# Tail of an MLP down projection: last token pair's products in another order, sample rows' norm first, one more row's affine on GpSimd, last row's norm from bn_stats moments

## The chip, the cores and the metric

The kernel runs on one core of one Trainium2 chip. The metric is device time in microseconds of one execution. A core has five engines that work side by side, each with its own queue of instructions in order: TensorE (PE, with its weight loads shown as PEld), VectorE (DVE), ScalarE (ACT), GpSimd (POOL) and SyncE (SP, which here issues the DMAs). They wait for each other through semaphores.

## The reference, cut to what matters

One layer of a streaming encoder for 1024 prompt rows and 64 sample rows of width 1024: a mixer of three head groups, a norm, and a squared-ReLU MLP with a second norm. The change touches only the end of the last line:

```python
def layer_norm(x, g, b):
    mu = jnp.mean(xf, axis=-1, keepdims=True)
    var = jnp.mean(jnp.square(xf - mu), axis=-1, keepdims=True)
    return ((xf - mu) * lax.rsqrt(var + LN_EPS) * g + b)
...
        h = jnp.square(jax.nn.relu(jnp.einsum('btd,df->btf', x, w_up)))
        xp = layer_norm(ALPHA * xp + h @ w_down, ln2_g[l], ln2_b[l])
```

The outputs concerned are y_prompt (1024 x 1024) and y_sample (64 x 1024), in float32.

## The kernel before, in words

The down projection multiplies the 4096 hidden features by w_down. The features are worked off in 16 groups g of 256. The 1024 prompt rows are eight tiles t of 128 rows, and a tile's sum stands in SBUF as acc[t, half], two halves of 512 columns. Tiles t and t + 4 form a pair, and a pair's two row tiles by two column halves are made of seven block products instead of eight (a Strassen-like scheme): the class Down has product(n) for n = 0 to 6, six matmuls of 128x128 by 128x512 each (L1715), with results in three PSUM banks named A, B and D. The tuple DOWN gives each product's bank: 0 A, 1 B, 2 A, 3 D, 4 A, 5 D, 6 A. Products in one bank add up, so a bank is read by evac(n) after each product, and the next product in the same bank has to wait until that read is done. evac(0) copies A to a tile p on ACT (L1732). evac(1) adds B and p to half 0 of tile i (its final value), evac(2) adds A to half 1 of i, evac(3) adds D to half 1 of i + 4, evac(4) finishes half 1 of i + 4, evac(5) half 1 of i, evac(6) half 0 of i + 4. The adds run on DVE (L1682). B starts from half 0 of tile i, copied there by preload() on ACT (L1703).

The last two groups, 14 and 15, form the tail. There are four Downs, ch[0] to ch[3]: ch[0] has tiles 0 and 4, ch[1] tiles 1 and 5 (group 14), ch[2] tiles 2 and 6, ch[3] tiles 3 and 7 (group 15). In the tail a final add is one instruction that also gives the row sums (L1725, a custom DVE operation and a short read of its accumulator). do(k, n) issues product n of ch[k] and its evac. h_split makes the high and low parts of a block of hidden features: per half of it two copies on ACT (L1421, L1425) and a subtraction on DVE (L1426).

When a tile is final, its norm follows. In order these are, by helper: neg_mean(t) on DVE (L1789); squares(t), a pass over 1024 columns on ACT with a sum (L1794) and then two small operations on POOL (L1784 and L1785, scale and offset, then the power -1/2); shift(t) on POOL (L1805). Then the affine, in one of two ways. normalize(t) on ACT (L1809), times(t) on POOL (L1813, by g) and plus(t) on POOL (L1817, plus b) with a DMA of the rows out (L1818). Or on_dve(t, i, step): for half i, step 0 is (y + (-mean)) * g (L1825) and step 1 is y * rstd + b with the DMA out (L1827, L1828), where g and b come from four PSUM tiles gbp that put_gb() fills on ACT (L1942). The sample rows are row tile NB = 8; fold(half) adds their two partial sums (L1950 on ACT, L1952 on DVE), moments are bn_stats (L1776) and scale does bn_aggr (L1781) and POOL operations (L1782, L1785), then shift (L1803).

The tail's order is written out by hand: the context in_order() ties each engine's instructions to the order in which the statements stand. So an instruction that waits holds back all that was written after it for its engine.

Which rows go which way before: tiles 8, 0, 4 and 1 wholly through ACT and POOL; of tile 2 columns 512 to 1023 and of tile 7 columns 768 to 1023 so; tiles 5, 6, 3 and the rest of 2 and 7 on DVE. ch[3] runs its products as 0, 1, 2, 3, 4, 5, 6.

## Time and profile before

| | us |
|---|---|
| time, median of 3 runs | 1411.81 (1410.02 to 1411.91) |
| time of the profiled execution | 1411.73 |
| its span, first to last instruction | 1410.0 |
| PE busy in the span | 1328.1 (94%) |
| DVE, ACT, POOL busy | 1002.6, 718.5, 602.3 |
| PE, DVE, ACT, POOL busy in the window 1385 to 1395 | 9.05, 7.63, 8.63, 8.51 |
| PE, DVE, ACT, POOL busy in the window 1400 to 1410 | 0.00, 5.92, 2.73, 3.59 |

The span is what the profile covers; the time of the same execution is 1.7 us longer. All places in time below are microseconds from the span's start. A row of the timeline gives the start of an instruction (or of several alike, with their count), its duration, engine, line and operation, what it writes and reads, and in square brackets how long its engine stood idle before it and which engine's instruction ended that. On the whole the kernel is bound by PE, but the tail is not: the last matmul ends some 11 us ahead of the span's end.

### The profile page before, as it was taken

Reading aid. Unit: us, or ns where it says so; the run is one execution under the profiler, and the core shown is the slowest. Engines: PE = TensorE matmul, PEld = TensorE weight load, DVE = VectorE, ACT = ScalarE, POOL = GpSimd, SP = SyncE. Lnnn points to the kernel's source line nnn. Section 1 sums busy time; section 2 is a strip of 40 time slices with the busy share of each in tenths; the row PEclk is TensorE's granted clock in tenths of the full one; section 3 lists DMA queues with packets and bytes.
Section 4 is the critical chain, followed back from the end, with each engine's and each line's share of the span. In section 5 each row is a group of like instructions: output and inputs, shape, how many; then the busy total and the mean of one; then the engine's idle time right before and its main releaser. Section 6 shows DMA issues by size and latency. Waiting matters only on the chain.

```text
span 1410.0 us, 24288 instructions
## 1 busy us (share of the span) xinstructions
PE 1328.1 (94%) x8827; PEld 1206.8 (86%) x8827; DVE 1002.6 (71%) x1799; ACT 718.5 (51%) x1561; POOL 602.3 (43%) x663
## 2 busy tenths in 40 slices
PE   7999999999989997999989999999979999999996
PEld 6899999999888986866889999999967787777774
DVE  3577565676786599887866768767678777667777
ACT  3366565666665485333423323232247667667675
POOL 3222222266565535654411122212166665654657
PEclk9999999999999998999999999999999999999999
DMA  7324242322313434422234434344558344344343
GB/s 218 77 78 113 58 117 65 81 63 56 80 27 83 127 91 135 132 105 68 76 110 140 153 133 139 117 166 139 173 187 295 99 160 165 118 136 150 101 135 128
DMA packets 149217, 168.87 MB, mean 120 GB/s; under 512 B 27100, under 2 KB 115484, under 8 KB 149096
## 3 DMA queue, kind: packets, MB, share of 16 engines
q1 hardware_dynamic: 149096, 167.30, 37.9%
q8 instruction: 70, 1.15, 0.3%
q14 instruction: 51, 0.42, 0.1%
HBM read 109.26 MB, written 51.71 MB: 114 GB/s over the span
## 4 chain that ended last, share of the span: by engine, by line
PE 63%; DVE 12%; ACT 7%; DMA 6%; POOL 6%; issue 5%; SPq 1%; DVEq 0%; ACTq 0%; POOLq 0%
PE zA L1264 9%; PE A L1715 6%; PE zD L1264 6%; PE mx L244 5%; PE kvsb L355 5%; PE kvfox L355 4%; PE D L1715 3%; PE zC L1264 3%; PE zB L1264 3%; DVE snsb L538 2%; DMA raw<-w_in 2%; PE qfox L496 2%; PE Sfox L554 2%; DMA rd<-w_down 2%; PE ptfox L602 1%
## 5 line engine op out<-in xcount | busy, mean ns | idle before, releaser
L97 POOL TENSOR_TENSOR wa<-wr,wa 128x512 fp32r<-128x512 f32 x42 | 63.8, 1548 | 228.5 <-ACT wa L1204 228.5
L97 POOL TENSOR_TENSOR wd<-rd,wd 128x512 fp32r<-128x512 f32 x77 | 101.1, 1322 | 121.2 <-ACT wd L1204 116.9
L244 PE MATMUL mx<-xT,oTb 128*128 128x512 f32 (+1 forms) x416 | 108.0, 412 | 1.6 <-ACT oTb L202 1.5
L1264 PE MATMUL zD<-xo,ws 128*128 128x288 f32 (+1 forms) x720 | 98.1, 289 | 0.6 <-DVE h4a L1426 0.3
L1264 PE MATMUL zA<-xo,ws 128*128 128x288 f32 (+1 forms) x720 | 98.1, 290 | 0.0
L244 PEld LDWEIGHTS mx<-xT,oTb 128*128 128x128 f32 (+1 forms) x416 | 78.1, 193 | 21.7 <-ACT oTb L202 2.5
L1264 PEld LDWEIGHTS zD<-xo,ws 128*128 128x128 f32 x720 | 93.7, 189 | 1.1 <-DVE h4a L1426 0.5
L1264 PEld LDWEIGHTS zA<-xo,ws 128*128 128x128 f32 x720 | 94.1, 189 | 0.1
L540 POOL TENSOR_TENSOR sgsb<-sgsb,snsb 128x127 f32<-128x127 f32 (+7 forms) x48 | 58.8, 1227 | 78.8 <-DVE snsb L538 64.3
L355 PE MATMUL kvfox<-wkvfox,xT 128*128 128x256 f32 (+3 forms) x624 | 90.6, 294 | 1.5 <-ACT wkvfox L331 0.5
L1204 ACT ACTIVATE wd<-rd 128x512 fp32r<-128x512 f32 x105 | 63.8, 624 | 51.6 <-DMA rd<-w_down 25.8
L355 PE MATMUL kvsb<-wkvsb,xT 128*128 128x256 f32 (+1 forms) x624 | 87.7, 286 | 0.0
L1715 PE MATMUL A<-wd,wd 128*128 128x512 f32 x312 | 83.0, 401 | 2.5 <-DVE acc L1682 2.3
L355 PEld LDWEIGHTS kvfox<-wkvfox,xT 128*128 128x128 f32 (+1 forms) x624 | 81.6, 193 | 3.3 <-DVE xT L97 1.0
L1396 POOL TENSOR_TENSOR rd<-rd 128x512 f32<-128x512 f32 x56 | 78.9, 1409 | 10.9 <-DVE b L97 8.7
L538 DVE TENSOR_TENSOR_SCAN snsb<-snsb,one 128x128 f32<-128x128 f32 (+7 forms) x48 | 72.2, 1507 | 13.3 <-ACT snsb L537 12.5
L1275 ACT ACTIVATE sn<-zA 128x256 f32<-128x256 f32 (+1 forms) x80 | 31.0, 390 | 98.4 <-PE zA L1264 82.6
L355 PEld LDWEIGHTS kvsb<-wkvsb,xT 128*128 128x128 f32 (+1 forms) x624 | 79.2, 187 | 0.2
L1715 PEld LDWEIGHTS A<-wd,wd 128*128 128x128 f32 x312 | 58.9, 191 | 18.9 <-DVE acc L1682 4.2
L1715 PE MATMUL A<-wd,h4a 128*128 128x512 f32 x240 | 65.1, 395 | 0.4 <-DVE acc L1682 0.3
L1478 ACT ACTIVATE ws<-wr 128x1024 fp32r<-128x1024 f32 x28 | 29.0, 1057 | 54.0 <-DVE wr L1214 54.0
L1715 PEld LDWEIGHTS A<-wd,h4a 128*128 128x128 f32 x240 | 44.5, 188 | 12.6 <-ACT p L1732 1.2
(537 smaller groups left out, 3746.2 us busy)
## 6 DMA issues: line engine op xcount, KB each, us to landing
h_dr<-hh SPq DMA_DIRECT2D x30, 512.0 KB, 3.2
rd<-w_down SPq DMA_DIRECT2D x30, 512.0 KB, 4.5
awa<-h_dr SPq DMA_DIRECT2D x30, 512.0 KB, 4.5
wr<-w_up SPq DMA_DIRECT2D x14, 1024.0 KB, 5.4
hr<-h_dr SPq DMA_DIRECT2D x32, 384.0 KB, 3.6
h_dr<-hh SPq DMA_DIRECT2D x30, 384.0 KB, 3.9
raw<-w_in SPq DMA_DIRECT2D x44, 256.0 KB, 3.3
xr<-x_prompt SPq DMA_DIRECT2D x8, 512.0 KB, 7.2
```

What stands on the lines that cost most here:

```text
L97: eng.tensor_tensor(out, src, hi.bitcast(F32), op=ALU.subtract)
L244: nc.tensor.matmul(acc[0:m], oT[:, k, hx, 0:m], wo[k // 4][hw][:, k % 4, cs], start=(i == 0), stop=(i == len(seq) - 1))
L355: nc.tensor.matmul(acc[0:n, c0:c0 + n1 - n0], xT[k // 4][:, k % 4, c:c + n], wt[:, k, hw, n0:n1], start=(i == 0), stop=(i == len(seq) - 1))
L496: nc.tensor.matmul(acc[:, 0:w], wq[:, k, hw, :], xT[k // 4][:, k % 4, c:c + w], start=(i == 0), stop=(i == len(seq) - 1))
L538: nc.vector.tensor_tensor_scan(g[:, 0:n][:, ::-1], g[:, 0:n][:, ::-1], one.broadcast_to([P, n]), 1.0, op0=ALU.mult, op1=ALU.bypass)
L540: nc.gpsimd.tensor_tensor(s[:, 0:n - 1], s[:, 0:n - 1], g[:, 1:n], op=ALU.mult)
L1204: nc.scalar.activation(hi, raw, AF.Copy)
L1264: nc.tensor.matmul(z, w[:, hw, k], xop(s, bo, hx)[:, k, :], start=(new and k == 0 and j == 0), stop=(k == 3 and j == 2), skip_group_check= ...
L1275: nc.scalar.activation(c, z, AF.Copy)
L1396: eng.tensor_tensor(r[:, o], r[:, x], r[:, y], op=ALU.subtract)
L1478: nc.scalar.activation(ws[:, 0, q, c], src[:, q], AF.Copy)
L1715: nc.tensor.matmul(z, h[:, hx, q, o], wset[self.c % 2][q][:, hw, wb], start=((n in (0, 3) or n == 1 and self.c == 0) and q == 0 and j == 0 ...
```

## The change

- ch[3] runs its products as 0, 3, 1, 2, 5, 4, 6, with the norm work of other tiles put at other places between them.
- The sample rows: fold, moments, scale and shift stand ahead of do(0, 3) instead of behind it and do(0, 4), and normalize, times and plus directly behind do(0, 4); the split of group 14's second block and the loads of group 15's second part come after the fold.
- Tile 0: normalize and times stand ahead of squares(4).
- Tiles 1 and 5: squares and normalize are placed earlier, among h_split's instructions. Tile 5 goes wholly through ACT and POOL (normalize, times, plus) instead of four on_dve steps, and put_gb() now stands behind normalize(5).
- Tile 3: columns 512 to 1023 go through normalize, times and plus instead of on_dve.
- Tile 7: its final adds are plain additions without row sums; instead of neg_mean and squares it has bn_stats per half on DVE, bn_aggr, and the POOL operations of the sample rows; on_dve then subtracts the mean.

```diff
             def last(self, at, z, other=None):
...
-                if self.sums is None:
+                if self.sums is None or t == NB - 1:
                     add(False, acc[at], z, other)
...
             if step == 0:
-                nc.vector.scalar_tensor_tensor(y, y, st[:, 12:13], gbp[i][:, 0:w], op0=ALU.add, op1=ALU.mult)
+                nc.vector.scalar_tensor_tensor(y, y, st[:, 12:13], gbp[i][:, 0:w],
+                                               op0=ALU.subtract if t == NB - 1 else ALU.add, op1=ALU.mult)
...
             do(0, 2)
-            h_split(g, 1, 1)
-            for q in range(2):
-                h_load(g + 1, 1, q)
-            do(0, 3)
             fold(0)
             fold(1)
-            do(0, 4)
-            h_split(g + 1, 0, 0)
             moments(NB, 0, TS)
             moments(NB, 1, TS)
             scale(NB, TS)
             shift(NB, TS, -1.0)
+            do(0, 3)
+            h_split(g, 1, 1)
+            for q in range(2):
+                h_load(g + 1, 1, q)
+            do(0, 4)
+            normalize(NB, TS)
+            times(NB, TS)
+            h_split(g + 1, 0, 0)
             ch[1].preload()
+            plus(NB, TS)
             do(0, 5)
             neg_mean(0)
             do(1, 0)
             h_split(g + 1, 0, 1)
+            squares(0)
+            shift(0)
             do(0, 6)
             neg_mean(4)
-            normalize(NB, TS)
-            times(NB, TS)
-            squares(0)
-            shift(0)
             do(1, 1)
-            plus(NB, TS)
+            normalize(0)
+            times(0)
             squares(4)
             shift(4)
-            normalize(0)
-            times(0)
             plus(0)
...
             do(2, 2)
+            squares(1)
+            shift(1)
             do(2, 3)
             h_split(g + 1, 1, 1)
-            squares(1)
-            shift(1)
+            normalize(1)
+            times(1)
             squares(5)
+            shift(5)
             ch[3].preload()
+            plus(1)
+            normalize(5)
+            times(5)
+            do(2, 4)
             put_gb()
-            do(2, 4)
-            on_dve(5, 0, 0)
             do(2, 5)
             neg_mean(2)
-            on_dve(5, 1, 0)
             do(3, 0)
-            normalize(1)
-            times(1)
-            on_dve(5, 0, 1)
-            on_dve(5, 1, 1)
             squares(2)
             shift(2)
             do(2, 6)
             neg_mean(6)
             squares(6)
-            plus(1)
+            plus(5)
+            do(3, 3)
+            on_dve(2, 0, 0)
+            do(3, 1)
+            on_dve(2, 0, 1)
             normalize(2, c0=512)
             times(2, c0=512)
+            do(3, 2)
             plus(2, c0=512)
-            do(3, 1)
-            on_dve(2, 0, 0)
-            do(3, 2)
-            on_dve(2, 0, 1)
-            do(3, 3)
             on_dve(6, 0, 0)
-            do(3, 4)
             on_dve(6, 0, 1)
-            on_dve(6, 1, 0)
             do(3, 5)
             neg_mean(3)
             squares(3)
+            shift(3)
+            on_dve(6, 1, 0)
             on_dve(6, 1, 1)
+            do(3, 4)
+            moments(7, 1)
+            on_dve(3, 0, 0)
+            on_dve(3, 0, 1)
+            normalize(3, c0=512)
             do(3, 6)
-            neg_mean(7)
-            squares(7)
-            for i in range(2):
-                for step in range(2):
-                    on_dve(3, i, step)
-            shift(7)
+            moments(7, 0)
+            scale(7)
+            shift(7, sign=-1.0)
+            times(3, c0=512)
             normalize(7, c0=768)
+            plus(3, c0=512)
+            on_dve(7, 0, 0)
+            on_dve(7, 1, 0, 768)
             times(7, c0=768)
             plus(7, c0=768)
-            for c0, c1 in ((0, 512), (512, 768)):
-                for step in range(2):
-                    on_dve(7, c0 // 512, step, c1)
+            on_dve(7, 0, 1)
+            on_dve(7, 1, 1, 768)
```

## The prediction, made before the changed kernel ran

> **What bounds the kernel now.** I read the page first, then the windows over the last 25 us, then the timeline of the tail engine by engine, because the diff only reorders and moves work there.
>
> ```profile
> span 1410.0 us, 24288 instructions
> 1385.00:1395.00 10.00, 9.05 (x40) 6.98 (x39) 7.63 (x18) 8.63 (x16) 8.51 (x13) 1.00 0.33 129
> 1400.00:1410.00 10.00, 0.00 (x0) 0.00 (x0) 5.92 (x11) 2.73 (x5) 3.59 (x8) 0.72 0.58 211
> ```
>
> The windows' columns are the busy time of PE, PEld, DVE, ACT and POOL. In 1385 to 1395 ACT (8.63) and POOL (8.51 of 10) are nearly as full as PE: there is little room on them. After 1400 PE has no work, so the time is set by the norms of the last tiles.
>
> ```profile
> 1392.11 1.56 PE L1715 MATMUL lastD<-wd,wd 128*128 128x512 f32 x6
> 1394.62 1.66 PE L1715 MATMUL A<-wd,wd 128*128 128x512 f32 x6 [0.94 <-DVE acc L1682]
> 1397.51 1.57 PE L1715 MATMUL A<-wd,wd 128*128 128x512 f32 x6
> 1399.84 0.69 DVE L1725 CUSTOM_DVE_ANT_0 acc<-A,acc 128x512 f32<-128x512 f32 x1
> 1402.50 0.74 DVE L1825 SCALAR_TENSOR_TENSOR acc<-acc,ident,gbp 128x512 f32<-128x512 f32 x1
> 1403.28 0.75 DVE L1827 SCALAR_TENSOR_TENSOR acc<-acc,ident,gbp 128x512 f32<-128x512 f32 x1
> 1403.94 0.74 DVE L1825 SCALAR_TENSOR_TENSOR acc<-acc,ident,gbp 128x512 f32<-128x512 f32 x1
> 1405.96 0.48 DVE L1827 SCALAR_TENSOR_TENSOR acc<-acc,ident,gbp 128x256 f32<-128x256 f32 x1
> 1405.61 0.33 SPq L1818 DMA_DIRECT2D y_prompt<-acc  x1
> 1406.06 0.85 SPq L1828 DMA_DIRECT2D y_prompt<-acc  x2
> ```
>
> The last product ends at 1399.08 (1397.51 + 1.57); DVE, behind with on_dve steps, takes its result only at 1399.84 and runs almost without a gap to 1406.44. The last DMA is issued at about 1406.5 (two issues from 1406.06, some 0.45 apart), and the span ends 3.5 later. So before, **DVE's queue** sets the end. An on_dve step takes 0.66 from start to start, or 0.78 behind its own tile's step (1402.50 to 1403.28).
>
> **The change part by part.** Its engines' orders follow the statements, so I walk the new order with the durations of the rows and look which engine arrives last.
>
> *The sample rows and the front.* fold and bn_stats now stand ahead of evac(3) of ch[0] on DVE, and normalize(8) ahead of two h_splits on ACT.
>
> ```profile
> 1363.27 0.68 DVE L1682 TENSOR_TENSOR acc<-acc,lastD 128x512 f32<-128x512 f32 x1
> 1363.87 1.27 DVE L1952 TENSOR_TENSOR acc<-acc,fold 64x512 f32<-64x512 f32 x2
> 1367.15 1.27 DVE L1776 BATCH_NORM_STATS2 lstb<-acc 64x6 f32<-64x512 f32 x2
> 1368.45 0.20 DVE L1781 BATCH_NORM_AGGREGATE lstb<-lstb 64x2 f32<-64x12 f32 x1
> 1370.20 1.23 ACT L1809 ACTIVATE acc<-acc,lstb 64x1024 f32<-64x1024 f32 x1
> 1362.34 1.01 DVE L1426 TENSOR_TENSOR wd<-hr,st 128x384 fp32r<-128x384 f32 x2
> 1362.91 0.84 SPq L1411 DMA_DIRECT2D hr<-h_dr  x2
> hr<-h_dr SPq DMA_DIRECT2D x32, 384.0 KB, 3.6
> 1380.28 0.52 ACT L1421 ACTIVATE wd<-hr 128x384 fp32r<-128x384 f32 x1
> ```
>
> Nothing is added, but two fold adds, two bn_stats and the aggregate (1.27 + 1.27 + 0.2, with a wait some 2.8) now lie ahead of that read of bank D, less 1.01 of h_split subtractions that move behind it: product 5 of ch[0] waits about 1.6. normalize(8), which waits for the POOL operations behind the aggregate, holds ACT's h_splits and the preload of ch[1] (another 0.5 to 0.6 on PE), and evac(2) of ch[1] comes 1 later. The same walk makes PE about 2.7 late when ch[3] starts. I cost this at **nothing**, because a longer wait of PE covers it (below); with that cover gone it would cost 2.3 to 2.7. POOL's stretch ends as before: tile 0's times starts 1.2 earlier, since normalize(0) stands ahead of squares(4), but tile 4's three small operations, 1.1, now come inside the stretch. The two loads that moved with the h_split keep their place in SP's queue, behind the ln2 loads and ahead of y_sample; issued some 4 later than 1362.91, they land (3.6) near 1371, long before ACT reads them at 1380.28 or later: nothing.
>
> *Tile 5 on POOL, and put_gb behind it.* This is the costly step.
>
> ```profile
> 1385.91 2.40 POOL L1817 TENSOR_TENSOR acc<-acc,gb 128x1024 f32<-128x1024 f32 x1
> 1388.39 0.19 POOL L1784 TENSOR_SCALAR ident<-ident 128x1 f32<-128x1 f32 x1
> 1388.67 0.55 POOL L1785 TENSOR_TENSOR ident<-ident,negh 128x1 f32<-128x1 f32 x1
> 1389.29 0.20 POOL L1805 TENSOR_TENSOR ident<-ident 128x1 f32<-128x1 f32 x1
> 1390.98 2.42 POOL L1813 TENSOR_TENSOR acc<-acc,gb 128x1024 f32<-128x1024 f32 x1 [0.58 <-ACT acc L1809]
> 1393.48 0.19 POOL L1784 TENSOR_SCALAR ident<-ident 128x1 f32<-128x1 f32 x1
> 1394.39 0.19 POOL L1805 TENSOR_TENSOR ident<-ident 128x1 f32<-128x1 f32 x1
> 1387.11 2.14 ACT L1942 ACTIVATE gbp<-gb 128x512 f32<-128x512 f32 x4
> 1389.19 0.58 ACT L1732 ACTIVATE p<-A 128x512 f32<-128x512 f32 x1
> 1389.67 1.23 ACT L1809 ACTIVATE acc<-acc,ident 128x1024 f32<-128x1024 f32 x1
> 1390.81 1.14 ACT L1794 ACTIVATE awa<-acc,ident 128x1024 f32<-128x1024 f32 x1
> 1393.22 0.75 DVE L1825 SCALAR_TENSOR_TENSOR acc<-acc,ident,gbp 128x512 f32<-128x512 f32 x1
> ```
>
> Before, POOL ends plus(4) at 1388.31, does tile 1's three small operations by 1389.49, ACT normalizes tile 1 from 1389.67, and times(1) starts at 1390.98. After, the same chain gives about the same start. But before, put_gb (1387.11) and p of ch[3] (1389.19) stood ahead of all that in ACT's queue; after, they stand behind normalize(5), which needs shift(5) on POOL, which stands behind times(1). So: times(1) ends 1393.4; tile 5's three small operations, as the ones from 1393.48 to 1394.58; normalize(5) from 1394.6, next in ACT's queue 1.14 later; put_gb at 1395.75; p of ch[3] 2.08 later (1387.11 to 1389.19) at 1397.8, against 1389.19; squares(2) 0.48 behind it at 1398.3, to 1399.45. Two waits hang on this. Product 2 of ch[3] may not write bank A until p is copied: PE stands about 3 us from product 1 to 1397.9, which is the cover named above. And on_dve(2, 0, 0) overwrites the tile that squares(2) reads, so it starts at about **1399.55 instead of 1393.22**, with DVE idle before it.
>
> *DVE from there.* The adds and bn_stats by rows above start 0.60 apart, 0.73 where the next needs the result; a summed add 0.61. In the new order: on_dve(2,0,0) 0.66, evac(1) 0.61, on_dve(2,0,1) 0.66, evac(2) 0.60, tile 6 half 0 0.78 + 0.66, evac(5) with its neg_mean 0.86, tile 6 half 1 0.78 + 0.66: 6.3, so evac(4) starts 1405.85. Product 6 follows product 4 in the same bank A, so PE waits for that read and runs 1406.6 to 1408.3. DVE goes on with 0.73 + bn_stats 0.60 + tile 3 half 0 0.78 + 0.66 and is at evac(6) at 1408.6, just behind PE; then 0.73, bn_stats 0.71, aggregate 0.3: POOL can start tile 7's small operations at **1410.35**.
>
> The four on_dve steps of tile 5 and two of tile 3 are gone from DVE (some 4.2), tile 7's neg_mean and two ACT passes are replaced by 1.3 of bn_stats and 0.2, but all of this saving lies behind a start 6.3 later. bn_stats on 128 partitions has no row; the 64-partition row is two in 1.27. Bounds are a third of that and twice that for each; I take the row, since the 64- and 128-partition rows of normalize (1.23 both) agree.
>
> *The end on POOL.*
>
> ```profile
> 1397.82 1.29 POOL L1813 TENSOR_TENSOR acc<-acc,gb 128x512 f32<-128x512 f32 x1
> 1399.19 1.27 POOL L1817 TENSOR_TENSOR acc<-acc,gb 128x512 f32<-128x512 f32 x1
> 1404.06 0.72 POOL L1813 TENSOR_TENSOR acc<-acc,gb 128x256 f32<-128x256 f32 x1 [0.71 <-ACT acc L1809]
> 1404.86 0.72 POOL L1817 TENSOR_TENSOR acc<-acc,gb 128x256 f32<-128x256 f32 x1
> ```
>
> times(3) and plus(3) stand behind tile 7's small operations in POOL's queue, and times(7), plus(7) behind them: 1.1 + 1.37 + 1.35 + 0.8 + 0.72 = 5.3, to 1415.65. DVE's last four steps (2.3) end by 1412.6 and do not matter. In SP's queue plus(7)'s DMA stands ahead of the two of on_dve(7), so the last issue is at 1415.7 + 0.9 = 1416.6, against 1406.5: **+10.1**. Walking the old order with these durations puts its end 0.4 late, so I take 0.4 off: +9.7. The profiled execution took 1411.73 (0.08 below the median): 1411.73 + 9.7 = **1421.4**.
>
> *The clock.* PE now stands twice for some 3 us.
>
> ```profile
> 639.83:643.24 3.41, 1.61 (x8) 0.85 (x6) 3.22 (x5) 1.09 (x2) 1.67 (x2) 0.99 0.44 156
> 643.24:646.65 3.41, 2.76 (x9) 2.37 (x10) 2.89 (x7) 0.72 (x2) 1.06 (x3) 0.50 0.36 90
> ```
>
> Here 3.41 us with PE busy for 1.61 are followed by 3.41 us at a granted clock of 0.50. The Trainium skill, TensorE: Matmul & The Clock Gate, Part 1, says the clock drops after an idle window of about 3.4 us; by that neither wait would do it and the sum stays. By the row, half an idle window does. Over products 2 and 5 of ch[3] half speed would hide behind DVE; over product 6 it costs up to 1.4 on PE, of which about 0.3 hides: +1.1.
>
> **The rivals.**
> 1. *POOL alone.* If put_gb does not hold ACT as I say, POOL's own queue stays: from times(1) at 1390.98 four passes of 2.48, six of 1.37 or less and 0.8 (1.37, 1.35, 1.37, 1.35, 0.8, 0.72) and some 5.5 of small operations: 22.4, less up to 0.8 where gaps close, end at 1412.6 to 1413.4; with two more issues about +7: 1418.7. For it: POOL is 8.51 of 10 busy even before. Against: ACT's queue is in order.
> 2. *Half clock over product 6*: +10.8, 1422.5. It depends on where the 3.41 us windows fall; about a third of the places do it.
> 3. *Faster: it does what it says.* If put_gb and p come by 1390.5, that is if normalize(5) does not have to wait for shift(5) behind times(1), DVE starts on time, without 4.2 of steps, and from evac(6) the end needs 0.73 + 0.71 + 0.3 + 2.3 = 4.0 instead of 6.6 (1399.84 to 1406.5): about -2.6, 1409.1. It decides at the moment put_gb starts: below 1390.5 faster, and every us above moves the end by as much. Against: the 1.23 + 2.42 + 1.1 ahead of it are rows; and rival 1 would still hold POOL.
> 4. *No change*: a gain like rival 3's and a loss on POOL cancel, 1411.7.
>
> **How the numbers follow.** Forecast 0.67, rival 1 0.12, rival 2 0.14, rival 3 0.04, rival 4 0.03. The range goes from 1417.0 (rival 1 less 1.7 for POOL starting its stretch earlier) to 1424.5 (rival 2 plus twice the time for three bn_stats, 1.9). A measurement of this kernel can tell about 0.2% from no change, 2.8 us: faster 0.04, same 0.03, slower 0.93.
>
> **What would show it.** In the changed profile: PE idle for about 3 us ahead of product 2 of ch[3], released by ACT's p; the gbp copies near 1395.8 behind a normalize that waits for POOL; DVE's first L1826 near 1399.5; tile 7's second bn_stats near 1409.5; POOL's last four passes behind the power of tile 7, and the last DMA issue near 1416.5. If the gbp copies start before 1392, or POOL's 1024-column passes take much less than 2.4, the prediction is wrong.

## The result, and the profile after

| | before | after |
|---|---|---|
| time, median | 1411.82 us (1410.02 to 1411.91, 4 runs) | 1419.93 us (1418.84 to 1420.54, 4 runs) |
| ratio, 95% interval | | 1.0059 [1.0045, 1.0074] |
| profiled execution: time, span | 1411.73, 1410.0 | 1420.54, 1418.8 |

The changed kernel is slower by 8.1 us in the medians, 6.4 to 10.4 by the interval. The forecast was 1421.4, in a range of 1417.0 to 1424.5.

Here are the same windows of the changed kernel's profile as were shown of before, with one more at the end (busy time of PE, PEld, DVE, ACT and POOL in each; then the granted clock, the DMA share and GB/s):

```profile
span 1418.8 us, 24283 instructions
1385.00:1395.00 10.00, 8.00 (x35) 6.11 (x33) 4.47 (x12) 6.19 (x10) 8.15 (x10) 1.00 0.13 53
1400.00:1410.00 10.00, 5.17 (x14) 3.31 (x12) 8.79 (x16) 2.06 (x3) 6.09 (x8) 0.78 0.48 184
1410.00:1419.00 9.00, 0.00 (x0) 0.00 (x0) 1.28 (x3) 0.60 (x1) 4.18 (x6) 0.57 0.25 88
```

In 1385 to 1395 every engine works less than before, POOL hardly (8.15 of 10 against 8.51), DVE (4.47 against 7.63) and ACT (6.19 against 8.63) much. Work that before lay beside the products lies behind them now: PE is busy for 5.17 after 1400, where it had no work, and the last window is POOL's. The timeline of the tail, all engines, shows where the time was lost:

```profile
1387.46 1.24 ACT L1809 ACTIVATE acc<-acc,ident 128x1024 f32<-128x1024 f32 x1 [1.71 <-POOL ident L1805]
1388.78 2.40 POOL L1813 TENSOR_TENSOR acc<-acc,gb 128x1024 f32<-128x1024 f32 x1 [1.35 <-ACT acc L1809]
1392.40 1.24 ACT L1809 ACTIVATE acc<-acc,ident 128x1024 f32<-128x1024 f32 x1 [2.07 <-POOL ident L1805]
1393.54 2.14 ACT L1944 ACTIVATE gbp<-gb 128x512 f32<-128x512 f32 x4
1395.62 0.57 ACT L1732 ACTIVATE p<-A 128x512 f32<-128x512 f32 x1
1396.25 1.83 PE L1715 MATMUL A<-wd,wd 128*128 128x512 f32 x6 [3.25 <-ACT p L1732]
1397.36 0.75 DVE L1826 SCALAR_TENSOR_TENSOR acc<-acc,ident,gbp 128x512 f32<-128x512 f32 x1 [5.04 <-ACT awa L1794]
1404.43 2.93 PE L1715 MATMUL A<-wd,wd 128*128 128x512 f32 x6 [2.18 <-DVE acc L1682]
1407.40 0.69 DVE L1682 TENSOR_TENSOR acc<-acc,A 128x512 f32<-128x512 f32 x1 [0.80 <-PE A L1715]
1409.14 0.23 POOL L1782 TENSOR_SCALAR ident<-ident 128x1 f32<-128x1 f32 x1 [3.50 <-DVE ident L1781]
1410.35 1.27 POOL L1813 TENSOR_TENSOR acc<-acc,gb 128x512 f32<-128x512 f32 x1
1413.72 0.72 POOL L1817 TENSOR_TENSOR acc<-acc,gb 128x256 f32<-128x256 f32 x1
1414.89 0.88 SPq L1830 DMA_DIRECT2D y_prompt<-acc  x2
```

Read it downward, bracket by bracket. times(1) on POOL (1388.78) holds tile 5's shift, for which normalize(5) on ACT waits (2.07, to 1392.40); behind it in ACT's queue come the gbp copies (1393.54) and p of ch[3] (1395.62). PE waits 3.25 for p, DVE 5.04 for squares(2). Then DVE is busy to the last product, and POOL, idle for 3.50 before tile 7's moments are there (1409.14), does its last four passes. The last DMAs are issued at the end of that.

**A measure for the parts.** Runs of one kernel differ by several us: before, in the 25 runs of one comparison, took 1406.47 to 1415.06. Nothing before the tail is changed, yet the last matmul into ds, the sample rows' sum, lies 1.64 earlier in after's execution. The first row is from the PE timeline of before, the second from that of after:

```profile
1359.90 0.40 PE L1761 MATMUL ds<-wd,hs 128*64 128x512 f32 x1
```

```profile
1358.26 0.40 PE L1761 MATMUL ds<-wd,hs 128*64 128x512 f32 x1
```

So beside each ratio I give the **stretch**: from the start of this matmul to the span's end, in the profiled execution. It is 1410.0 - 1359.90 = 50.10 before and 1418.8 - 1358.26 = 60.54 after: **+10.44**. That is above the +8.1 of the medians; the 1.64 of the unchanged part is most of the difference. The stretch is one execution of each kernel, and how much it differs between executions of one kernel was not measured; differences of half a us in it are read with that in mind. Places inside it repeat well where the statements are alike: in the seven kernels with the new front, product 5 of ch[0] starts 5.74 or 5.75 from the matmul, and in the four that have times(1) where the changed kernel has it, that starts at 30.45 to 30.52. Places "from the matmul" below are counted from its start.

### The profile page after: what moved, and what is told of

It is laid out like the page before. It is cut to its first block, busy times and chain, and to the rows that moved or that the text cites. A ratio compares the mean times of both kernels' runs of the same rounds, so it can differ in the third digit from the quotient of the medians.

```text
span 1418.8 us, 24283 instructions
## 1 busy us (share of the span) xinstructions
PE 1330.5 (94%) x8827; PEld 1209.4 (85%) x8827; DVE 1002.1 (71%) x1793; ACT 720.2 (51%) x1561; POOL 610.5 (43%) x669
## 3 DMA queue, kind: packets, MB, share of 16 engines
q8 instruction: 70, 1.15, 0.4%
## 4 chain that ended last, share of the span: by engine, by line
PE 61%; DVE 11%; ACT 7%; DMA 7%; POOL 6%; issue 5%; SPq 1%; POOLq 0%; ACTq 0%; DVEq 0%
PE zA L1264 9%; PE zD L1264 6%; PE A L1715 6%; PE kvsb L355 5%; PE mx L244 5%; PE kvfox L355 4%; PE zC L1264 3%; PE zB L1264 3%; PE D L1715 2%; DMA rd<-w_down 2%; PE qfox L496 2%; PE Sfox L554 2%; DVE snsb L538 2%; POOL wd L97 1%; DMA awa<-h_dr 1%
## 5 line engine op out<-in xcount | busy, mean ns | idle before, releaser
L1682 DVE TENSOR_TENSOR acc<-acc,A 128x512 f32<-128x512 f32 x75 | 50.4, 679 | 8.0 <-PE A L1715 8.0
```

Source lines behind the costliest of these rows:

```text
L1682: nc.vector.tensor_tensor(out, out if other is None else other, bank, op=ALU.add)
```

## The experiments

All results first; each ratio is against before, run on the same chip in the same comparison.

| kernel | median us (runs) | ratio [95%] | matmul at, span | stretch | less before's |
|---|---|---|---|---|---|
| tile5_on_dve | 1417.27 (8) | 1.0055 [1.0035, 1.0075] | 1363.81, 1420.4 | 56.59 | +6.49 |
| gb_and_squares_first | 1421.71 (6) | 1.0086 [1.0060, 1.0112] | 1359.76, 1420.1 | 60.34 | +10.24 |
| front_only | 1413.56 (12) | 1.0024 [1.0009, 1.0040] | 1358.93, 1411.0 | 52.07 | +1.97 |
| order_only | 1414.84 (12) | 1.0030 [1.0013, 1.0046] | 1361.20, 1413.6 | 52.40 | +2.30 |
| moments_tile3 | 1413.87 (11) | 1.0020 [1.0008, 1.0032] | 1359.93, 1411.9 | 51.97 | +1.87 |
| pe_kept_busy | 1420.76 (5) | 1.0065 [1.0053, 1.0077] | 1358.04, 1417.7 | 59.66 | +9.56 |
| after_work_order | 1414.43 (12) | 1.0019 [1.0008, 1.0030] | 1362.20, 1416.0 | 53.80 | +3.70 |
| order_searched | 1410.17 (12) | 0.9997 [0.9981, 1.0013] | 1359.76, 1408.2 | 48.44 | -1.66 |
| old_front | 1422.60 (6) | 1.0072 [1.0058, 1.0086] | 1358.76, 1419.2 | 60.44 | +10.34 |
| moments_only | 1411.65 (12) | 0.9997 [0.9983, 1.0011] | 1357.99, 1408.6 | 50.61 | +0.51 |
| hold_alone | 1421.65 (4) | 1.0076 [1.0049, 1.0103] | 1363.50, 1422.2 | 58.70 | +8.60 |
| pool_alone | 1419.33 (6) | 1.0065 [1.0041, 1.0089] | 1360.00, 1418.3 | 58.30 | +8.20 |

By their times alone, tile5_on_dve, gb_and_squares_first, pe_kept_busy, old_front, hold_alone and pool_alone cannot be told from the changed kernel (1.0059 [1.0045, 1.0074]): the intervals overlap. What is said of these six rests on the stretches and the rows.

The theory is the forecast's: tile 5 on POOL, with put_gb and p of ch[3] held behind it, costs the time. Its rivals are POOL's queue alone, and the half clock over the last product.

### Tile 5 back on DVE

The changed kernel, with tile 5's four on_dve steps and put_gb ahead of normalize(1) as before:

```diff
             h_split(g + 1, 1, 1)
-            normalize(1)
-            times(1)
             squares(5)
-            shift(5)
             ch[3].preload()
-            plus(1)
-            normalize(5)
-            times(5)
-            do(2, 4)
             put_gb()
+            do(2, 4)
+            on_dve(5, 0, 0)
             do(2, 5)
             neg_mean(2)
+            on_dve(5, 1, 0)
             do(3, 0)
+            normalize(1)
+            times(1)
+            on_dve(5, 0, 1)
+            on_dve(5, 1, 1)
...
             squares(6)
-            plus(5)
+            plus(1)
```

> The changed kernel with one part undone: tile 5 goes back to DVE (four on_dve steps), and put_gb and p of ch[3] stand ahead of normalize(1) again. My theory (tile 5 on POOL, with ACT waiting for it, is the costly step): put_gb starts about 3.5 us earlier than in the changed kernel, DVE's first step of tile 2 some 3 us earlier, and the time is about 3.3 us below the changed kernel's, some 5 to 6 above before. Rival (the loss is in the front, in the product order or in the clock): within 1 us of the changed kernel.

The stretch is 56.59: 3.95 of the 10.44 go. From the timeline of this kernel (ACT; and PE for the matmul):

```profile
1363.81 0.40 PE L1761 MATMUL ds<-wd,hs 128*64 128x512 f32 x1
1392.89 2.15 ACT L1944 ACTIVATE gbp<-gb 128x512 f32<-128x512 f32 x4
```

The gbp copies start 29.08 from the matmul, against 35.28 in the changed kernel, 6.2 earlier; the end comes 3.95 earlier. The last product runs at half clock here as in the changed kernel (2.93 in both PE timelines), so the clock is not mixed into this difference. By the stretch, tile 5's way is the largest of the parts tried singly, but +6.49, more than half of the loss, is left of other parts. This edit takes away both the two passes on POOL and the hold on ACT, and cannot say which of them counted; the next three kernels ask that.

### The hold taken away: put_gb and squares(2) first

The changed kernel with tile 5 still on POOL, but with put_gb and squares(2) ahead of normalize(5):

```diff
             h_split(g + 1, 1, 1)
-            normalize(1)
-            times(1)
             squares(5)
-            shift(5)
             ch[3].preload()
-            plus(1)
-            normalize(5)
-            times(5)
-            do(2, 4)
             put_gb()
+            do(2, 4)
             do(2, 5)
             neg_mean(2)
             do(3, 0)
+            normalize(1)
+            times(1)
+            shift(5)
             squares(2)
...
             squares(6)
+            plus(1)
+            normalize(5)
+            times(5)
             plus(5)
```

> The changed kernel with tile 5 left on POOL, but ACT's copies put_gb and p, and the squares of tiles 2 and 6, stand ahead of normalize(5) and do not wait for it. Two readings of my prediction part here. If the hold of ACT behind POOL is what costs (its step 'put_gb behind normalize(5)'), DVE starts tile 2 about 4 us earlier and the end comes 3 to 4 us earlier. If POOL's queue itself is the limit (rival 1), tile 2's and 3's small operations on POOL only move behind tile 1's and 5's passes, DVE waits for them instead, and the time is the changed kernel's or up to 1.5 us more. By the sum of rows I expect the second.

The stretch is 60.34, only 0.20 shorter. The timeline of this kernel, ACT, POOL and DVE:

```profile
1388.84 2.15 ACT L1944 ACTIVATE gbp<-gb 128x512 f32<-128x512 f32 x4
1392.71 2.41 POOL L1813 TENSOR_TENSOR acc<-acc,gb 128x1024 f32<-128x1024 f32 x1 [2.88 <-DVE ident L1789]
1393.80 0.75 DVE L1826 SCALAR_TENSOR_TENSOR acc<-acc,ident,gbp 128x512 f32<-128x512 f32 x1
1407.43 0.55 POOL L1785 TENSOR_TENSOR ident<-ident,negh 128x1 f32<-128x1 f32 x1
1408.02 0.75 DVE L1829 SCALAR_TENSOR_TENSOR acc<-acc,ident,gbp 128x512 f32<-128x512 f32 x1 [4.67 <-POOL ident L1785]
```

DVE starts its on_dve steps at 1393.80, 34.04 from the matmul, against 39.10 in the changed kernel: 5.06 earlier. It loses it again: its step 1 of tile 3 waits 4.67 for tile 3's power on POOL (L1785, 1407.43), which stands behind all passes of tiles 1, 5 and 2. But the edit is not clean. It also put normalize(1) behind put_gb and p, POOL stood idle for 2.88, and times(1) started 32.95 from the matmul (1392.71 - 1359.76) in place of 30.52. So 0.20 is no measure of the hold: up to 2.43 of it may be hidden by this second delay.

### The hold alone, with tile 1 left in its place

Here normalize(1) and times(1) stay where the changed kernel has them, and only put_gb, p and squares(2) come ahead of normalize(5):

```diff
             squares(5)
             shift(5)
             ch[3].preload()
+            put_gb()
             plus(1)
-            normalize(5)
-            times(5)
             do(2, 4)
-            put_gb()
             do(2, 5)
             neg_mean(2)
             do(3, 0)
             squares(2)
+            normalize(5)
+            times(5)
             shift(2)
```

> The changed kernel with put_gb, p of ch[3] and squares(2) ahead of normalize(5) on ACT, and normalize(1) and times(1) left where they are (in gb_and_squares_first they came later, so that times(1) started 2.43 later from the last sample matmul than in the changed kernel: 1392.71 - 1359.76 = 32.95 against 1388.78 - 1358.26 = 30.52, and POOL stood idle for 2.88; that made its 0.20 an unclean measure of the hold). Expected by the walk with the rows of the changed kernel: gbp copies about 1390.3, p 1392.4, DVE's first on_dve of tile 2 about 1394.1, that is 35.9 from the matmul in place of 39.10; times(5) 0.8 later. If the hold on ACT sets the time: the stretch falls by the whole 3.2 that DVE starts earlier, to about 57.3. If POOL's queue is a limit close behind it: DVE waits for tile 3's power on POOL (L1785) ahead of its step 1 of tile 3, and the stretch falls by 0.5 to 1.2 only, to about 59.6.

The stretch is 58.70, 1.84 shorter than the changed kernel's: between what the two theories gave. Its timeline, DVE (the matmul is at 1363.50):

```profile
1399.26 0.75 DVE L1826 SCALAR_TENSOR_TENSOR acc<-acc,ident,gbp 128x512 f32<-128x512 f32 x1 [1.70 <-ACT awa L1794]
1404.24 0.75 DVE L1829 SCALAR_TENSOR_TENSOR acc<-acc,ident,gbp 128x512 f32<-128x512 f32 x1 [1.41 <-POOL ident L1785]
1410.05 0.75 DVE L1829 SCALAR_TENSOR_TENSOR acc<-acc,ident,gbp 128x512 f32<-128x512 f32 x1 [0.79 <-POOL ident L1785]
```

DVE starts at 35.76 (1399.26 - 1363.50), 3.34 earlier than in the changed kernel. Then it waits 0.21, 1.41 and 0.79 for POOL's power of a tile, behind whole passes, and so gives back 2.41. In return it no longer stands idle 0.80 for the last product, though that runs at half clock here too (2.86). That leaves 3.34 - 2.41 + 0.80 = 1.73, close to the 1.84 that reach the end.

### POOL's queue by itself

As hold_alone, and tile 3's two steps on DVE stand behind tile 7's moments:

```diff
-            on_dve(3, 0, 0)
-            on_dve(3, 0, 1)
             normalize(3, c0=512)
             do(3, 6)
             moments(7, 0)
             scale(7)
+            on_dve(3, 0, 0)
+            on_dve(3, 0, 1)
```

> As hold_alone, and on DVE tile 3's two steps stand behind tile 7's moments, so that DVE waits for POOL nowhere before tile 7's moments and POOL does not wait for them behind it: what is left is POOL's queue by itself, the rival that was priced at +7 (stretch 57.1). If that price is right: stretch about 57.6 (POOL's passes of tiles 5 and 2 end about 1405.2 by the changed kernel's rows, tile 3's and 7's small operations 1.1 each, then four passes of 4.2), 2.9 shorter than the changed kernel's 60.54. If POOL needs more than its passes say (the rival's price too low), the stretch stays at 59.5 or more.

The stretch is 58.30, +8.20, 0.40 shorter than hold_alone's; 57.6 was expected if the rival's price is right. DVE did still wait for POOL, 1.40 ahead of tile 6's step 1, which the expectation had left out. From its timeline, PE, DVE and POOL (times(1) first):

```profile
1390.47 2.40 POOL L1813 TENSOR_TENSOR acc<-acc,gb 128x1024 f32<-128x1024 f32 x1 [1.36 <-ACT acc L1809]
1404.46 2.42 PE L1715 MATMUL A<-wd,wd 128*128 128x512 f32 x6 [4.04 <-DVE acc L1682]
1406.91 0.69 DVE L1682 TENSOR_TENSOR acc<-acc,A 128x512 f32<-128x512 f32 x1 [1.78 <-PE A L1715]
1408.66 0.23 POOL L1782 TENSOR_SCALAR ident<-ident 128x1 f32<-128x1 f32 x1 [1.85 <-DVE ident L1781]
1413.23 0.72 POOL L1817 TENSOR_TENSOR acc<-acc,gb 128x256 f32<-128x256 f32 x1
```

The last product is late behind evac(4), runs in part at half clock (2.42), DVE waits 1.78 for it, and POOL 1.85 for tile 7's moments. From times(1) at 1390.47 to the end of its last pass at 1413.95 POOL takes 23.48, or 21.63 without those 1.85; the rival had priced this at 22.4 less up to 0.8. So POOL's queue was priced rightly, and it does not stand alone: with the 1.85 this kernel is at +8.20. What it would be without them, +6.35, is an estimate by subtraction that no kernel shows.

### One part at a time, on the kernel before

Four kernels do one part of the change each, starting from before. **The front alone**: the statements of the changed kernel up to do(1, 2) (the diff's first half, in the change's section), and before's from there.

```diff
             do(0, 2)
-            h_split(g, 1, 1)
-            for q in range(2):
-                h_load(g + 1, 1, q)
-            do(0, 3)
             fold(0)
             fold(1)
-            do(0, 4)
-            h_split(g + 1, 0, 0)
             moments(NB, 0, TS)
...
+            do(0, 3)
+            h_split(g, 1, 1)
```

> The kernel before with the front of the change alone (sample rows' norm first, tile 0's normalize ahead of squares(4)); from do(1, 2) on it is the kernel before. With no 3 us wait of PE to cover it, my price for this part is 2.3 to 2.7 us above before. Rival (it is free, since its operations were only moved): within 0.5 us of before. A second rival (POOL gets the sample rows out of the way early, so it gains): 1 to 2 us below before.

Stretch +1.97, time 1.0024 [1.0009, 1.0040]. Its PE timeline has three waits that the front's forecast named or implied:

```profile
1364.67 1.66 PE L1715 MATMUL lastD<-wd,wd 128*128 128x512 f32 x6 [1.15 <-DVE acc L1682]
1369.57 1.65 PE L1715 MATMUL lastB<-wd,h4b 128*128 128x512 f32 x6 [0.47 <-ACT lastB L1703]
1375.21 1.66 PE L1715 MATMUL A<-wd,wd 128*128 128x512 f32 x6 [1.27 <-DVE acc L1682]
```

Product 5 of ch[0] waits 1.15 for evac(3) behind the sample rows' sums, the first product into ch[1]'s B 0.47 for the preload, and a product in ch[1]'s A 1.27 for evac(2).

**The product order alone**: before, with ch[3]'s products as 0, 3, 1, 2, 5, 4, 6 and all norm statements where they were.

```diff
             plus(2, c0=512)
-            do(3, 1)
+            do(3, 3)
             on_dve(2, 0, 0)
-            do(3, 2)
+            do(3, 1)
             on_dve(2, 0, 1)
-            do(3, 3)
+            do(3, 2)
             on_dve(6, 0, 0)
-            do(3, 4)
             on_dve(6, 0, 1)
...
             on_dve(6, 1, 1)
+            do(3, 4)
             do(3, 6)
```

> The kernel before with only ch[3]'s products in the new order 0, 3, 1, 2, 5, 4, 6. Product 6 then follows product 4 in bank A, and PE must wait for DVE's read between them. My theory: about 2 us above before, with PE's last product some 2.5 us later and idle ahead of it. Rival (the new order removes the wait of 0.94 ahead of product 4 and only moves it): within 0.5 us of before.

Stretch +2.30, time 1.0030 [1.0013, 1.0046]. The PE timeline of this kernel shows the price: products 4 and 6, both in bank A, now stand together at the end.

```profile
1401.44 1.95 PE L1715 MATMUL A<-wd,wd 128*128 128x512 f32 x6 [2.63 <-DVE ident L1725]
```

This is product 6: it waits 2.63 until DVE has read product 4 out of A. Before it started 37.61 from the matmul (1397.51 - 1359.90), here 40.24 (1401.44 - 1361.20).

**Tile 7's moments and tile 3's second half on POOL**: before, with the work of the changed kernel's last part in it. The statements stand close to the changed kernel's order but not quite in it, since the products keep before's: here tile 3's steps come behind scale(7). (L1722 and L1825 as in the change's diff.)

```diff
             squares(3)
+            shift(3)
             on_dve(6, 1, 1)
+            moments(7, 1)
             do(3, 6)
-            neg_mean(7)
-            squares(7)
-            for i in range(2):
-                for step in range(2):
-                    on_dve(3, i, step)
-            shift(7)
+            moments(7, 0)
+            scale(7)
+            on_dve(3, 0, 0)
+            on_dve(3, 0, 1)
+            normalize(3, c0=512)
+            times(3, c0=512)
+            shift(7, sign=-1.0)
             normalize(7, c0=768)
+            plus(3, c0=512)
             times(7, c0=768)
```

> The kernel before with the last part of the change alone: tile 7 by bn_stats moments and plain adds, tile 3's columns 512 to 1023 through ACT and POOL, with the old product order, tile 5 on DVE and the old front. My theory: DVE ends a little earlier (two on_dve steps less, two bn_stats more), but POOL's four last passes come behind tile 7's small operations and end the kernel: 1.8 us above before in the stretch from the last sample matmul to the end. With the three parts already run (tile 5 3.9, front 2.0, order 2.3 in that stretch) the four would add up to 10.0 of the measured 10.4. Rival (the moments shorten the last chain, as two ACT passes go): 1 to 2 us below before.

Stretch +1.87, time 1.0020 [1.0008, 1.0032]. The timeline of its last us, DVE and POOL:

```profile
1405.56 0.48 DVE L1829 SCALAR_TENSOR_TENSOR acc<-acc,ident,gbp 128x256 f32<-128x256 f32 x1
1406.72 0.72 POOL L1817 TENSOR_TENSOR acc<-acc,gb 128x256 f32<-128x256 f32 x1
```

DVE ends at 1406.04, 46.11 from the matmul, a little ahead of before (1406.44 - 1359.90 = 46.54). POOL, which in before ended at 1405.58 (1404.86 + 0.72), 45.68 from it, ends at 1407.44, 47.51 from it. The work left DVE, and the end went with it to POOL.

**Tile 7's moments alone**, in the same way but with tile 3 wholly on DVE:

```diff
             on_dve(6, 1, 1)
+            moments(7, 1)
             do(3, 6)
-            neg_mean(7)
-            squares(7)
+            moments(7, 0)
+            scale(7)
+            shift(7, sign=-1.0)
+            normalize(7, c0=768)
             for i in range(2):
                 for step in range(2):
                     on_dve(3, i, step)
-            shift(7)
-            normalize(7, c0=768)
             times(7, c0=768)
```

> The kernel before with tile 7's norm by bn_stats moments alone (plain adds, two bn_stats, bn_aggr, subtract in on_dve), tile 3 on DVE as before. It takes two ACT passes' wait off POOL's chain for tile 7 but puts two bn_stats (0.6 each) on DVE, which sets the end there: 1 us above before in the stretch. If the chain over ACT set the end, it would be about 1 us below before.

Stretch +0.51, time 0.9997 [0.9983, 1.0011], which cannot be told from no change. The end stays on DVE (timeline, DVE; POOL's last pass ends at 1403.78):

```profile
1405.03 0.48 DVE L1829 SCALAR_TENSOR_TENSOR acc<-acc,ident,gbp 128x256 f32<-128x256 f32 x1
```

DVE's last step ends at 1405.51, 47.52 from the matmul: 0.98 later than before, with two bn_stats and an aggregate added to the engine that sets the end. Of this the span shows 0.51; the rest lies behind the last DMA issue, from which the span's end is 3.06 away (1405.54, SP's timeline) against 3.5 before. There the last two issues are 0.91 apart, in before some 0.45; that this is the reason is not shown. By difference, 1.36 of the 1.87 belong to tile 3's second half on POOL.

### The old front in the changed kernel

The changed kernel with before's statements up to do(1, 2): the front's part undone. It tells whether the front's 1.97 is paid in the change as well.

```diff
             do(0, 2)
+            h_split(g, 1, 1)
+            for q in range(2):
+                h_load(g + 1, 1, q)
+            do(0, 3)
             fold(0)
             fold(1)
+            do(0, 4)
+            h_split(g + 1, 0, 0)
             moments(NB, 0, TS)
...
-            do(0, 3)
-            h_split(g, 1, 1)
```

> The changed kernel with the front put back: sample rows' norm and tile 0 as in the kernel before, everything from do(1, 2) on as changed. My prediction priced the front at nothing here, because PE's longer wait ahead of product 2 covers it: then the stretch from the last sample matmul to the end stays at the changed kernel's 60.5 within 0.5 us. If instead the parts simply add up (front alone cost 2.0), the stretch is 58.5.

Stretch 60.44, 0.10 below the changed kernel's. Two rows of the kernel's timeline, PE and DVE:

```profile
1397.13 2.93 PE L1715 MATMUL A<-wd,wd 128*128 128x512 f32 x6 [4.18 <-ACT p L1732]
1398.24 0.75 DVE L1826 SCALAR_TENSOR_TENSOR acc<-acc,ident,gbp 128x512 f32<-128x512 f32 x1 [7.80 <-ACT awa L1794]
```

PE, which no longer comes late, waits 4.18 for p in place of 3.25: this is the cover. The 0.10 is no clean price, since half clock fell on this product and not on the last (1.66), as it did in the changed kernel; the next experiment prices that at 0.88. The places ahead of the last product say it without the clock: times(1) starts 30.93 from the matmul (1389.69 in POOL's timeline; the matmul is at 1358.76) and DVE's first step 39.48, against 30.52 and 39.10 in the changed kernel. So within the change the new front does not delay the chain; it brings it some 0.4 earlier.

### PE kept busy in its waits

The changed kernel with 12 spare matmuls behind product 1 of ch[3] and 7 behind product 4, into a PSUM tile that nobody reads: work that the reference does not have, so that PE does not stand still.

```diff
+        def fill(z, n):
+            h = h_tile(2 * c + 1, 0, 1)
+            for k in range(n):
+                nc.tensor.matmul(z, h[:, 0, 0, k % 4], wset[c % 2][0][:, 0, 0],
+                                 start=True, stop=True, skip_group_check=True)
...
             do(3, 1)
+            spare = ps.tile([P, 512], F32, name="spare", tag="acc", bufs=2)
+            fill(spare, 12)
...
             do(3, 4)
+            fill(spare, 7)
```

> The changed kernel with extra matmuls that nobody reads, into a bank that is free by then: 12 behind product 1 of ch[3] and 7 behind product 4, so that PE does not stand idle there. They add work that the reference does not have. If the half clock comes from PE's waits (rival 2, the granted clock in the profile), product 6 takes about 1.7 us instead of 2.93 and the stretch from the last sample matmul to the end is 0.8 us shorter than the changed kernel's. If the half clock has another cause, product 6 stays at 2.9 or the extra matmuls only delay it, and the stretch is the same or up to 1 us longer.

First what the clock did in the changed kernel, in windows of 3.41 us (PE's busy time is the first number behind the length, the granted clock the third from the end):

```profile
1390.77:1394.18 3.41, 2.23 (x10) 1.47 (x8) 1.07 (x4) 1.78 (x3) 3.17 (x5) 1.00 0.01 2
1394.18:1397.59 3.41, 1.34 (x6) 1.12 (x7) 0.23 (x1) 3.38 (x7) 2.99 (x3) 1.00 0.40 159
1397.59:1401.00 3.41, 3.41 (x10) 2.65 (x9) 3.31 (x7) 1.77 (x3) 2.99 (x6) 0.50 0.00 0
1401.01:1404.42 3.41, 1.24 (x6) 0.68 (x4) 3.30 (x8) 1.24 (x2) 3.33 (x3) 1.00 0.50 196
1404.42:1407.83 3.41, 2.93 (x6) 1.84 (x6) 2.51 (x4) 0.81 (x1) 0.98 (x4) 0.50 0.82 303
```

A window with PE busy for 1.34 and one with 1.24 are each followed by one at 0.50; the one with 2.23 is not. The second of the slow windows holds the last product, which took 2.93. With PE kept busy, the PE timeline reads:

```profile
1392.63 2.96 PE L1959 MATMUL spare<-wd,wd 128*128 128x512 f32 x12
1396.03 1.67 PE L1715 MATMUL A<-wd,wd 128*128 128x512 f32 x6 [0.44 <-ACT p L1732]
1401.31 1.80 PE L1959 MATMUL spare<-wd,wd 128*128 128x512 f32 x7
1404.21 1.67 PE L1715 MATMUL A<-wd,wd 128*128 128x512 f32 x6 [1.11 <-DVE acc L1682]
```

The last product takes 1.67, the granted clock is 1.00 in all five windows from 1390.56 to 1407.60, and the stretch is 59.66, 0.88 shorter. That is nearly the 0.80 that DVE stood idle for product 6 in the changed kernel (1407.40 there). In the time, 1.0065 [1.0053, 1.0077] against 1.0059 [1.0045, 1.0074], so small a gain does not show; that the half clock comes from PE's waits, and what it costs in the tail, rests on the rows.

### The same work in another order

Is it the work on POOL or the order of the statements? This kernel issues the instructions of the changed kernel (tile 5 and half of tile 3 through POOL, tile 7 by moments) with the statements of the whole tail in another order. The diff is long; a piece of it:

```diff
             squares(5)
-            shift(5)
+            do(3, 0)
+            do(2, 2)
+            do(2, 5)
+            neg_mean(2)
+            do(3, 3)
+            h_split(g + 1, 1, 1)
+            do(3, 2)
+            do(3, 4)
+            do(2, 4)
             ch[3].preload()
+            do(3, 1)
+            normalize(0)
             plus(1)
+            do(3, 5)
+            shift(5)
+            squares(2)
+            times(0)
             normalize(5)
             times(5)
```

> The changed kernel's work on the changed kernel's engines, instruction for instruction, but its tail's statements in another order, put together by walking the queues with the rows' durations so that no engine waits that need not. If the order of the change is the fault, this comes out at or below before. If the work on POOL is (tile 5's two passes and tile 3's), it stays above before: I expect some 5.9 us less than the changed kernel, still 3 to 4 above before.

Stretch 53.80: 6.74 of the 10.44 go by order alone, and 3.70 stay. The time shows it too: 1.0019 [1.0008, 1.0030], clear of the changed kernel's 1.0045 to 1.0074. So, measured against before as it is, most of the loss is not work that has to be done but its order; a better order than this one may exist. How much work came to POOL, its groups show, from the matmul's place to the end; the first fence is from before, the second from after (busy us, mean ns of one, and idle time ahead):

```profile
L1813 POOL TENSOR_TENSOR acc<-acc,gb 128x1024 f32<-128x1024 f32 (+3 forms) x5 | 9.2, 1848 | 2.8 <-ACT acc L1809 2.8
L1817 POOL TENSOR_TENSOR acc<-acc,gb 128x1024 f32<-128x1024 f32 (+3 forms) x5 | 9.2, 1841 | 0.2
```

```profile
L1813 POOL TENSOR_TENSOR acc<-acc,gb 128x1024 f32<-128x1024 f32 (+3 forms) x7 | 12.9, 1838 | 2.7 <-ACT acc L1809 2.7
L1817 POOL TENSOR_TENSOR acc<-acc,gb 128x1024 f32<-128x1024 f32 (+3 forms) x7 | 12.8, 1830 | 0.4
```

Two passes more in each group, 3.7 + 3.6 = 7.3 us, on the engine that was already 8.51 of 10 busy in 1385 to 1395.

### Before's work in another order

Before's instructions (tile 5 and all of tile 3 on DVE), with the statements of the tail in another order too. A piece of the diff against before:

```diff
+            do(3, 2)
+            on_dve(5, 0, 1)
+            ch[3].preload()
             squares(6)
-            plus(1)
-            normalize(2, c0=512)
-            times(2, c0=512)
-            plus(2, c0=512)
-            do(3, 1)
             on_dve(2, 0, 0)
-            do(3, 2)
-            on_dve(2, 0, 1)
             do(3, 3)
             on_dve(6, 0, 0)
+            do(3, 1)
+            normalize(1)
+            on_dve(2, 0, 1)
             do(3, 4)
```

> The kernel before, the same instructions on the same engines, its tail's statements in another order found by the same walk: evacs ahead of norm steps on DVE, squares on ACT ahead of normalize where normalize would wait for POOL, product 1 of ch[1] and ch[2] later. If orders walked on rows can be trusted, the stretch from the last sample matmul to the end is about 2.5 us shorter than before (1409 or so in time). Rival (waits that the walk leaves out take it back): within 0.5 us of before or above it.

The window of this kernel beside which before's 9.05 is to be read:

```profile
1385.00:1395.00 10.00, 10.00 (x45) 8.04 (x44) 9.60 (x23) 7.09 (x11) 9.18 (x13) 1.00 0.35 136
```

In this window PE stands still no more, and the stretch is 48.44, 1.66 shorter than before's, where 2.5 was expected. The time is 0.9997 [0.9981, 1.0013]: no version is shown to beat before. The 1.66 would be 0.12%, which this measurement cannot tell from nothing. Beside after_work_order it is the fairer comparison of the work, each in an order of its own: 53.80 - 48.44 = 5.36 us for the work that the change moves. That rests on the stretches, since the intervals of the two times still overlap a little, and neither order is known to be the best for its work.

## Why the prediction was right, step by step

The time and its sign were right, and most places in the tail came as forecast. From the matmul, forecast then measured: times(1) 31.08, 30.52; the gbp copies 35.85, 35.28; p 37.9, 37.36; DVE's first on_dve of tile 2 39.65, 39.10; evac(6) 48.7, 49.14; tile 7's small operations on POOL 50.45, 50.88.

- **The front.** Right in mechanism and in its claim. In the changed kernel product 5 of ch[0] waited 1.15 (forecast 1.6) and ch[1]'s preload 0.44 (0.5 to 0.6). These rows of its PE timeline are the same waits as in the front alone:

```profile
1364.00 1.67 PE L1715 MATMUL lastD<-wd,wd 128*128 128x512 f32 x6 [1.15 <-DVE acc L1682]
1368.89 1.67 PE L1715 MATMUL lastB<-wd,h4b 128*128 128x512 f32 x6 [0.44 <-ACT lastB L1703]
```

  PE started ch[3] 2.37 later than before (28.98 against 26.61 from the matmul), where 2.7 was forecast. Alone the front cost 1.97 where 2.3 to 2.7 were forecast for the case without cover, and within the change it delays nothing on the chain, as said. "POOL's stretch ends as before" was 0.56 off: times(1) came that much earlier, and with it the whole chain behind it; old_front shows that some 0.4 of this is the front's own doing.

- **"Tile 5 on POOL, and put_gb behind it. This is the costly step."** The waits are there, with the releasers that were forecast: PE 3.25 for p, where about 3 was forecast, and DVE 5.04 for squares(2), so that its first step of tile 2 starts 5.78 later than before from the matmul, where 6.3 was forecast. Tile 5's way as a whole is the largest part tried singly: 3.95. But the forecast hung its whole +9.7 on this step, and +6.49 stays when it is undone. What failed is how the hold was counted, as rival 3 put it: "every us above moves the end by as much". With the hold taken away DVE started 3.34 earlier, and 1.84 of that reached the end, because POOL's small operations, behind its passes, were late next. So of the loss the hold carries about 1.8, and +8.60 stands without it. The sum came out all the same, as far as can be told because its walk carried every queue along in the new order, the other late ones too; it is the weight given to the hold alone that was too great.

- **Rival 1, POOL alone, +7.** Not what the changed kernel shows first, but what lies close behind. Its queue was priced about right (21.63 from times(1) on without the idle time, against 21.6 to 22.4), but the kernel that leaves it alone is at +8.20. Its price added up POOL's passes and left out that DVE and POOL wait for each other in turn: DVE for a tile's power, POOL for tile 7's moments.

- **The clock, rival 2.** It came true together with the forecast, not instead of it. The last product ran at half clock and took 2.93; removing that took 0.88 off, where +1.1 were forecast. The trace's row (half an idle window can be enough) was the right one to weigh. The Trainium skill, TensorE: Matmul & The Clock Gate, Part 1, speaks of an idle window of about 3.4 us; here windows in which PE was busy for 1.34 and 1.24 of 3.41 us were followed by half speed, so the measurement decides. Without the half clock the forecast gave a stretch of 50.10 + 9.7 = 59.8, and the kernel without it measured 59.66. With it, rival 2 gave 50.10 + 10.8 = 60.9, and the changed kernel measured 60.54: in the stretch rival 2, with its chance of 0.14, was nearer than the forecast.

- **bn_stats on 128 partitions**, taken at the 64-partition row, was right:

```profile
1404.41 0.69 DVE L1776 BATCH_NORM_STATS2 ident<-acc 128x6 f32<-128x512 f32 x1
```

- **What the sum did not price by itself.** The product order costs 2.30 on its own, and the moments with tile 3's half on POOL 1.87. The walk through the queues held both within its waits. The four parts taken singly (3.95 for tile 5, undone; 1.97, 2.30 and 1.87, done alone) add to 10.09, close to 10.44, but that is no proof that they add: the front, 1.97 alone, is shown not to delay the chain within the change. Each part makes one engine late, and the latest hides the rest.

- **1421.4 against a median of 1419.93.** The stretch was forecast 59.8 and came 60.54; the unchanged part ahead lay 1.64 earlier than in before's execution. The sum came out of one execution, and such a shift is not in it. So the nearness of the time is in part luck: a chain 0.56 early, a half clock that cost 0.88 and this 1.64 partly cancel.

Rivals 3 and 4, faster and no change, are excluded by the interval 1.0045 to 1.0074. What stays open: how much of the loss an order better than that of after_work_order would still take back, and why, with the moments alone, the span ends sooner behind the last DMA issue. A hold on ACT without tile 5's passes on POOL was not tried.

## What to carry to other kernels

Before moving work to an engine that is off the path, add up what it has in the stretch and look at what stands behind each of its instructions: POOL was 85% busy, and four more passes put the small operations that DVE and ACT wait for behind them. The wait that a trace names pays only down to what is late next: remove it alone, and change nothing else in doing so. With queues in order, the same instructions differed by 6.74 us by the order of the statements, so a change of work should be judged with its order searched again.

## What the hardware showed that I had not expected

- Half speed of PE for one 3.41 us window, after a window in which it was busy for 1.24 to 1.34 us: six 128x512 float32 products took 2.93 us in place of 1.67. Nineteen spare matmuls in the waits removed it. The trace of before bears it out. Cut from 639.83 in both directions into windows of 3.413 us, on which its half-speed stretches fall, it shows this from 10 us to the last matmul: ten windows at full speed had PE busy for 1.75 or less and were followed by half speed, two were not (at 295.1 with about 1.7, and the last, at 1397.5, with 1.56), and none with 1.9 or more was. So about half a window decides in this kernel, and not sharply.
- Runs of before lay between 1405.42 and 1415.30 us in one comparison, and the start of the tail, in single executions of kernels that are the same up to there, between 1357.99 and 1363.81. A change of 2 us needs either many runs or a mark inside the trace.
